# Feed-forward layers in seven stretches instead of five, with 26 instead of 22 row pairs of half B multiplied by slabs

## The chip, the cores and the metric

The kernel runs on one core of one Trainium2 chip. The metric is the time of one execution in microseconds on the device. The engines are called as in the profile: PE (matmul; PEld is its weight load), DVE (vector), ACT (scalar), POOL (GpSimd) and SP (Sync, which here only issues DMAs).

## What is computed

A decoder trunk of two layers for 256 tokens of width 2048, in float32. Each layer has a mixer and then a feed-forward part; this case is about the feed-forward part, which takes two thirds of the time:

```python
def squared_relu_mlp(h, w1, w2):
    z = jax.nn.relu(h @ w1)          # (256 x 2048) @ (2048 x 8192)
    return (z * z) @ w2              # (256 x 8192) @ (8192 x 2048)

for i in range(DEPTH):               # DEPTH = 2
    ...
    x = x + squared_relu_mlp(rms_norm(x, ffn_norm[i]), w_ff1[i], w_ff2[i])
```

Every float32 operand is split into a rounded high part and a rest, and a product is formed as high x high + high x low + low x high. So each matmul of the mathematics is three on PE, and each weight that arrives needs one copy on ACT (the high part, line 178) and one subtraction on DVE (the low part, line 181).

## The kernel before

`ffn(l, ...)` computes the feed-forward part of layer `l`. Tokens stand in two tiles of 128, the hidden width 8192 in 64 chunks of 128, taken in 32 pairs.

**The up projection** has 64 tiles `("f", j)`, one a chunk (`up_tile`). A tile takes 16 weight blocks of 128 x 128. A block is one matmul 512 wide (high weights with both parts of the input, line 947) and one 256 wide (low weights, line 949). When both tiles of a pair are there, `convert` squares and splits them over the next ticks (`STEPS`; a tick is 4 blocks) and forms sums of them.

**The down projection** is done in two ways. The 2048 output columns fall into half A (the upper 1024) and half B (the lower 1024).

- *By slabs* (`slab_jobs`): for one pair and one half, a two by two scheme with seven products instead of eight. A product is three matmuls 512 wide (lines 1038 to 1040), so a pair is 21 matmuls, dealt out in four jobs with 2, 1, 2 and 2 products. The two weight rows of a pair (512 KB each, loaded by SP) are combined on the way: POOL issues a DMA that adds half of the second row to the first, DVE does one subtraction (line 209) and one sum (line 212). The seven products add up in seven PSUM banks over a whole stretch.
- *Directly* (`down_tile`): 8 tiles `("d", 3, n)` of 128 columns, blocks as in the up projection. It covers the pairs from `NB` on in half B, so each tile has 2 x (32 - 22) = 20 blocks. `add_down` scales and adds each tile's result with three DVE operations 256 wide (lines 967 to 969).

All 32 pairs of half A and the first `NB` of half B go by slabs. `PHASES` cuts this work into stretches, each with one half and a range of pairs. At a stretch's end `finish_banks` empties the seven banks with two ACT copies and seven DVE operations 512 wide, into four corners. What an earlier stretch of the same half left is added by `gather` (DMAs on POOL) and, if more is to come, stored in HBM by `park` (SP). The last sum of a half is scaled on ACT (`scale`), transposed on PE in four steps (`turn`, tile `ct`) and added to the residual by DVE (line 1119).

**Order.** `ffn_plan` writes the order out by hand: before each tile come up to `room` jobs of the current stretch (2 in the first stretch and in the first two gaps of each later one, then 4), as far as their pairs are ready, four tiles after their second up tile (`LAG`). In the last eight tiles `room` is 4 as well. `at(d, fn)` runs a function d ticks later.

**Loads.** `Feed` prepares weights up to `AHEAD` = 3 jobs before their use and loads three rows beyond that. Direct rows go through four `raw` buffers, slab rows through three `rows` buffers and, during the stage, two that the residual's tiles lend (`feed.more`: `residb`, `residc`): the residual is stored to HBM (`kept`) at the start of the stage and brought back (`reload`) in the last stretch, when no slab is in them any more. `resida`, twice as large, lends its space to two more spots for the hidden chunks (16 + 2 `spots`). SP works off its DMAs in order, so one that waits holds all behind it.

Of the kernel before, what the change touches and what calls it, by code (L numbers as in the profile page):

```python
# [18 lines left out]
P = 128  # L19
T = 256  # L20
# [85 lines left out]
class Feed:  # L106


    def __init__(self, tc, wst, wpool, rows, plan, dry):
# [9 lines left out]
        self.more, self.lent, self.turn = [], [], 0  # L119
# [6 lines left out]
    def load(self, upto):  # L126
        while self.lp < min(upto, len(self.plan.loads)):
# [6 lines left out]
            else:  # L134
                self.turn += 1
                c = self.turn % 5
                if self.more and c > 2:
                    pool, tag = self.more[c - 3]
                    self.lent.append(r)
# [45 lines left out]
    def _prepare(self, p):  # L185
# [27 lines left out]
        if p[2] == 3:  # L213
            for r in (("S", p[1], 0), ("S", p[1], 1)):
                del self.raw[r]
                if r in self.lent:
                    self.lent.remove(r)
# [77 lines left out]
NB = 22  # L295
PHASES = (("A", 0, 6), ("B", 0, 12), ("A", 6, 18), ("B", 12, 22), ("A", 18, 32))


def ffn_plan(tiles):
# [14 lines left out]
    for t, what in enumerate(tiles):  # L314
        room = 2 if phase == 0 or since < 2 else 4
        if t >= len(tiles) - 8:
            room = 4
        since += 1
        first = len(items)
        while jobs and room and ready[jobs[0][1]] <= t and jobs[0][0] == phase:  # L320
            items.append(("s", *jobs.pop(0)))
            room -= 1
            if not jobs or jobs[0][0] != phase:
                items.append(("end", phase))
                if PHASES[phase][2] == NB:
                    turns = {t + 7 + h: h for h in range(4)}
# [37 lines left out]
def program(ctx, tc, plan, dry, xT, memT, par, lam, cst, wst, yT):  # L364
# [55 lines left out]
    def resid_part(i, name):  # L420
        if i == "a":
            both = sp.tile([P, 8, T], F32, tag="resida", name=name)
            return [both[:, 0:4, :], both[:, 4:8, :]]
        return [sp.tile([P, 4, T], F32, tag=f"resid{i}", name=name)]

    resid = Halves([x for i in "abc" for x in resid_part(i, f"resid{i}")], 4)
# [411 lines left out]
    def ffn(l, xs, tag, done):  # L838
# [19 lines left out]
        def reload(first, tags):  # L858
            for i in tags:
                for x in resid_part(i, f"resid{i}{l}"):  # L860
                    resid.parts[first] = x
                    nc.sync.dma_start(x, kept[:, 4 * first : 4 * first + 4, :])
                    first += 1

        feed.more = [] if dry else [(sp, "residb"), (sp, "residc")]
        more = sp.tile([P, 4, 512], F32R, tag="resida", name=f"more{l}")
        spots += [more[:, 2 * j : 2 * j + 2, :] for j in range(2)]
# [3 lines left out]
        def take(late):  # L871
            s = min(x for x in spare if x < 16 or not late)
            spare.remove(s)
            return s
# [20 lines left out]
        def convert(i, late):  # L895
# [16 lines left out]
            def high():  # L912
                zat[i] = take(i >= 20)
# [14 lines left out]
            def sums_high():  # L928
                sat[i] = take(i > 20)
# [122 lines left out]
        part, turns = {}, []  # L1052

        def finish_banks(p):
# [4 lines left out]
            if p == len(PHASES) - 1:  # L1059
# [22 lines left out]
            if p == len(PHASES) - 1:  # L1082
                sides = ((upp, slice(0, 2)), (low, slice(2, 4)))
            old = part.pop(half, None)
# [8 lines left out]

# [696 lines left out]
```

## Time and profile before

| | us |
|---|---|
| median of 3 runs | 2015.45 (2015.44 to 2015.52) |
| profiled execution | 2016.58, of which span 2014.8 |
| up to the first feed-forward part | 252.4 |
| feed-forward of layer 0 (252.4 to 931.2) | 678.8; DVE busy 614.9, ACT 466.8 |
| between (931.2 to 1330.4) | 399.2; DVE busy 316.8, ACT 275.8 |
| feed-forward of layer 1 (1330.4 to 2010.5) | 680.1; DVE busy 612.2, ACT 462.4 |

The granted clock of PE is 1.00 in every stretch asked for. A row of the order of time reads: start, duration, engine, line, operation, output<-input, shape, count; in brackets stands idle time before it and what ended it. Matmuls overlap, so the distance of two starts, not the duration, is what one costs. A row of a window reads: its limits and length, then the busy time of each engine with its count of instructions, the granted clock, the mean busy share of the DMA engines and GB/s. A row of the waits reads: who waited for whom, us in total, how many times, the longest.

### The profile page before, as it was taken

What the parts mean: (1) busy time and instruction counts of PE and PEld (TensorE: products, weight loads), DVE (VectorE), ACT (ScalarE), POOL (GpSimd) and SP (SyncE); (2) the same over time, 40 slices, a digit from 0 to 9 for tenths busy, and PEclk for the clock granted to TensorE, in tenths of its full rate; (3) what the DMA queues carried; (4) which work ended last, traced back from release to release, by engine and by line L of the source; (5) the groups of instructions that cost most, each with busy time, mean ns of one, the idle gap of its engine ahead of it and who ended that gap; (6) DMA issues with size and microseconds to landing.
All of it is one profiled execution on the core that took longest, in us unless ns stands there. A gap on an engine that the chain in (4) does not pass through costs nothing.

```text
span 2014.8 us, 30584 instructions
## 1 busy us (share of the span) xinstructions
PE 2003.7 (99%) x10636; PEld 1709.2 (85%) x10636; DVE 1754.6 (87%) x2665; ACT 1371.6 (68%) x2209; POOL 163.3 (8%) x191
## 2 busy tenths in 40 slices
PE   9999999999999999999999999999999999999999
PEld 7888888888888888888888889888888888888887
DVE  8888778999999999998775698878899999999987
ACT  7765467676666677667665698557676677677664
POOL 0001300000001110000000000320000000101000
PEclk9999999999999999999999999999999999999999
DMA  9566767777878888756656545666777877878775
GB/s 310 183 195 201 231 205 214 239 226 227 247 230 241 250 224 264 214 180 214 227 183 195 187 143 174 216 222 213 234 233 221 247 223 231 264 232 240 243 214 157
DMA packets 135370, 442.95 MB, mean 220 GB/s; under 512 B 15344, under 2 KB 18416, under 8 KB 135216
## 3 DMA queue, kind: packets, MB, share of 16 engines
q1 hardware_dynamic: 117216, 406.39, 60.4%
q0 software_dynamic: 17856, 34.61, 10.4%
q8 instruction: 83, 1.36, 0.3%
q14 instruction: 71, 0.58, 0.1%
q10 hardware_dynamic: 144, 0.01, 0.0%
HBM read 425.61 MB, written 12.58 MB: 217 GB/s over the span
## 4 chain that ended last, share of the span: by engine, by line
PE 55%; DVE 1%; DMA 1%; ACT 1%; issue 0%; POOL 0%; ACTq 0%; DVEq 0%; POOLq 0%
PE x_bank L947 13%; PE x_bank L949 6%; PE p L1038 5%; PE p L1040 5%; PE p L1039 5%; PE wo L522 3%; PE k L553 3%; PE v L553 3%; PE q L553 3%; PE ff L947 2%; PE wo L524 1%; PE mv L553 1%; PE mk L553 1%; PE ff L949 1%; DMA c_b<-part 1%; DVE lo_ring L181 1%
## 5 line engine op out<-in xcount | busy, mean ns | idle before, releaser
L181 DVE TENSOR_TENSOR lo_ring<-raw,hi_ring 128x512 fp32r<-128x512 f32 (+1 forms) x685 | 570.1, 847 | 128.4 <-ACT hi_ring L178 121.3
L178 ACT CAST hi_ring<-raw 128x512 fp32r<-128x512 f32 (+1 forms) x685 | 497.5, 741 | 231.4 <-PE wo L522 67.2
L181 DVE TENSOR_TENSOR lo_ring<-slab,hi_ring 128x1024 fp32r<-128x1024 f32 (+1 forms) x324 | 334.5, 1042 | 48.9 <-ACT hi_ring L178 47.3
L178 ACT CAST hi_ring<-slab 128x1024 fp32r<-128x1024 f32 (+1 forms) x324 | 293.5, 907 | 112.9 <-DVE slab L212 56.9
L149 POOL DMA_DIRECT2D slab<-in_w x108 | 93.6, 867 | 1575.9 <-DVE lo_ring L181 468.8
L947 PE MATMUL x_bank<-fx,hi_ring 128*128 128x512 f32 x664 | 209.2, 395 | 0.0
L522 PE MATMUL wo<-cat,hi_ring 128*128 128x512 f32 x512 | 161.6, 396 | 0.0
L178 ACT CAST slot<-slab 128x1024 fp32r<-128x1024 f32 x108 | 113.4, 1050 | 68.0 <-PE x_bank L947 62.8
L181 DVE TENSOR_TENSOR slot<-slab,slot 128x1024 fp32r<-128x1024 f32 x108 | 131.8, 1220 | 21.7 <-ACT slot L178 21.2
L949 PEld LDWEIGHTS x_bank<-fx,lo_ring 128*128 128x128 f32 x664 | 124.7, 188 | 29.4
L947 PE MATMUL x_bank<-fx0b,hi_ring 128*128 128x512 f32 x472 | 148.2, 395 | 0.0
L961 ACT COPY room<-x_bank 128x512 f32<-128x512 f32 x118 | 68.9, 584 | 99.2 <-PE x_bank L949 99.1
L212 DVE TENSOR_TENSOR slab<-slab,slab 128x1024 f32<-128x1024 f32 x108 | 131.6, 1218 | 0.4
L949 PE MATMUL x_bank<-fx,lo_ring 128*128 128x256 f32 x664 | 130.8, 278 | 0.0
L524 PEld LDWEIGHTS wo<-cat,lo_ring 128*128 128x128 f32 x512 | 96.0, 188 | 22.0
L949 PEld LDWEIGHTS x_bank<-fx0b,lo_ring 128*128 128x128 f32 x472 | 88.7, 188 | 21.0
L947 PEld LDWEIGHTS x_bank<-fx,hi_ring 128*128 128x128 f32 x664 | 103.0, 189 | 2.2
L524 PE MATMUL wo<-cat,lo_ring 128*128 128x256 f32 x512 | 101.7, 278 | 0.0
L178 ACT CAST slot<-raw 128x1024 fp32r<-128x1024 f32 (+1 forms) x76 | 74.1, 976 | 28.6 <-PE x_bank L947 21.9
L181 DVE TENSOR_TENSOR slot<-raw,slot 128x1024 fp32r<-128x1024 f32 (+1 forms) x76 | 85.9, 1132 | 8.0 <-ACT slot L178 7.9
L949 PE MATMUL x_bank<-fx0b,lo_ring 128*128 128x256 f32 x472 | 92.7, 278 | 0.0
L947 PE MATMUL x_bank<-fx0a,hi_ring 128*128 128x512 f32 x280 | 88.0, 395 | 0.0
(561 smaller groups left out, 4787.9 us busy)
## 6 DMA issues: line engine op xcount, KB each, us to landing
raw<-in_w SPq DMA_DIRECT2D x508, 512.0 KB, 4.5
slab<-in_w SPq DMA_DIRECT2D x216, 512.0 KB, 3.8
slab<-in_w POOLq DMA_DIRECT2D x108, 256.0 KB, 5.0
part<-room SPq DMA_DIRECT2D x6, 512.0 KB, 4.7
kept<-resida SPq DMA_DIRECT2D x4, 512.0 KB, 4.6
room<-part POOLq DMA_DIRECT2D x4, 512.0 KB, 8.6
resida<-kept SPq DMA_DIRECT2D x4, 512.0 KB, 7.5
memraw<-in_mem SPq DMA_DIRECT2D x4, 512.0 KB, 3.9
```

What stands on the lines that cost most here:

```text
L149: self.nc.gpsimd.dma_start(t[:, 512:1024], self.wst[other, :, 512:1024], accum_op=ALU.add)
L178: cast = self.nc.scalar.copy(hi, src)
L181: self.nc.vector.tensor_sub(lo, src, hi.bitcast(F32))
L212: add(two, t.unsqueeze(1).to_broadcast([P, 2, 512]), two)
L522: nc.tensor.matmul(ps, hi, xs[:, k, :], start=first and j == 0, stop=False)
L524: nc.tensor.matmul(ps[:, T : 2 * T], lo, xs[:, k, 0:T], start=False, stop=last and j == len(ks) - 1,)
L553: nc.tensor.matmul(ps[t], a, b, start=i == 0 and j == 0, stop=i == NK - 1 and j == 2)
L947: nc.tensor.matmul(ps, hi, src(k), start=k == ks[0], stop=False)
L949: nc.tensor.matmul(ps[:, T : 2 * T], lo, src(k)[:, 0:T], start=False, stop=k == ks[-1])
L1038: nc.tensor.matmul(ps, al, hi[:, s], start=i == begin, stop=False)
L1039: nc.tensor.matmul(ps, ah, hi[:, s], start=False, stop=False)
L1040: nc.tensor.matmul(ps, ah, lo[:, s], start=False, stop=i == end - 1)
```

## The change

It does the following.

1. `NB` goes from 22 to 26: four more pairs of half B by slabs; the eight direct tiles shrink from 20 to 12 blocks.
2. `PHASES` has seven stretches instead of five, with 2 to 11 pairs each; half A and half B alternate as before.
3. `room` becomes 5 instead of 4 in every second gap before an up tile, from the third gap of a stretch on.
4. The residual's tiles are four of one size (`resida` to `residd`), and all four lend their space: seven slab buffers in turn. The two extra `spots` go. Before the last stretch a and b are taken out of the turn; in it a, b and later c, d are brought back.
5. Half A, parked for the last time by the third stretch from the end, is scaled before it is parked. In the last stretch the parked sum is loaded into two free spots (`fetched`, SP), and two fused DVE operations 1024 wide scale the new sum and add the parked one, in place of a gather by POOL and a scaling on ACT. The four turns come 7 to 10 ticks after the stretch's end instead of 13 to 16.
6. The turns of half B stand before tiles 60 to 63.
7. Behind layer 0 the later squares run one a tick instead of two, the statistics they feed at tick 36 instead of 28, and the splits of `x_mx` every third tick from 50 on instead of every second from 30 on.

```diff
-                c = self.turn % 5
-                if self.more and c > 2:
+                c = self.turn % (3 + len(self.more))
+                if c > 2:
...
-NB = 22
-PHASES = (("A", 0, 6), ("B", 0, 12), ("A", 6, 18), ("B", 12, 22), ("A", 18, 32))
+NB = 26
+PHASES = (
+    ("A", 0, 2), ("B", 0, 6), ("A", 2, 11), ("B", 6, 16), ("A", 11, 21), ("B", 16, 26), ("A", 21, 32)
+)
+LAST = len(PHASES) - 1
...
         room = 2 if phase == 0 or since < 2 else 4
-        if t >= len(tiles) - 8:
-            room = 4
+        if room == 4 and since % 2 and what[0] == "f":
+            room = 5
...
-        feed.more = [] if dry else [(sp, "residb"), (sp, "residc")]
-        more = sp.tile([P, 4, 512], F32R, tag="resida", name=f"more{l}")
-        spots += [more[:, 2 * j : 2 * j + 2, :] for j in range(2)]
+        feed.more = [] if dry else [(sp, f"resid{i}") for i in "abcd"]
...
-            old = part.pop(half, None)
+            old = part.pop(half, None) if p < LAST else None
...
+            if p == LAST:
+                for t, side in enumerate((upp, low)):
+                    stt(
+                        side, side, r2c[0][:, t : t + 1], fetched[t].bitcast(F32),
+                        ALU.mult, ALU.add,
+                    )
+                for h in range(4):
+                    at(7 + h, lambda h=h: turn(h))
                 return
-            at(11, scale)
-            for h in range(4):
-                at(13 + h, lambda h=h: turn(h))
+            if old is not None:
+                at(10, gather)
+            if not whole:
...
+                at(6 if old is None else 17, park)
+                if p == LAST - 2:
+                    at(15, scale)
+                return
...
+                    if (p, i, j) == (LAST - 1, NB - 2, 3):
+                        feed.more = feed.more[2:]
+                    if (p, i, j) == (LAST, 23, 3):
+                        reload("ab")
+                    if (p, i, j) == (LAST, 28, 3):
                         feed.more = []
-                    if (p, i, j) == (4, 31, 1):
-                        assert not feed.lent
-                        reload(2, "bc")
+                        for t in range(2):
+                            fetched.append(spots[take()])
+                            nc.sync.dma_start(
+                                fetched[t].bitcast(F32), part["A"][:, 2 * t : 2 * t + 2, :]
+                            )
+                    if (p, i, j) == (LAST, 31, 1):
+                        reload("cd")
...
-        at(18 + n // 2, lambda n=n: later_square(n))
+        at(18 + n, lambda n=n: later_square(n))
...
-        at(30 + 2 * n, lambda n=n: split_gain(x_mx[:, n, :], resid[:, n, :], gcol(G_MIX + 16 + n)))
+        at(50 + 3 * n, lambda n=n: split_gain(x_mx[:, n, :], resid[:, n, :], gcol(G_MIX + 16 + n)))
```

Where instructions move, at three places.

First SP, at the end of the last stretch of layer 0; `raw` and `slab` are weight rows, `resid..<-kept` brings the residual back. Before:

```order
L147 DMA raw_7794<-in_w 128x1024
L862 DMA residb_7966<-kept_2627 128x1024
L147 DMA raw_7870<-in_w 128x1024
L862 DMA residc_7968<-kept_2627 128x1024
L147 DMA raw_7889<-in_w 128x1024
L147 DMA slab_7820<-in_w 128x1024
L147 DMA raw_7891<-in_w 128x1024
```

And now:

```order
L147 DMA slab_7866<-in_w 128x1024
L147 DMA slab_7922<-in_w 128x1024
L147 DMA raw_7951<-in_w 128x1024
L862 DMA residc_8038<-kept_2628 128x1024
L147 DMA raw_7963<-in_w 128x1024
L147 DMA raw_7965<-in_w 128x1024
L147 DMA raw_7985<-in_w 128x1024
L862 DMA residd_8040<-kept_2628 128x1024
```

Before, the last slab row stood behind the reloads; now the last slab rows stand ahead of them, and only direct rows behind. The reloads of a and b and the two fetches of the parked sum stand further up in the same stretch, among slab and direct rows.

Second DVE, at the end of the last stretch of layer 0, from the third seventh-part operation on; `c_a` and `c_b` are the corners, `p_..` the banks, `lo_ring` and `slot` the low parts of weights. Before:

```order
L1074 TENSOR_TENSOR c_b<-c_a,p_6727 128x512
L1075 TENSOR_TENSOR c_a<-c_a,p_6729 128x512
L1076 TENSOR_TENSOR c_a<-c_a,c_b 128x512
L181 TENSOR_TENSOR lo_ring<-raw_7891,hi_ring 128x512
L1077 TENSOR_TENSOR c_a<-c_a,p_6730 128x512
L1078 TENSOR_TENSOR c_b<-c_b 128x512
L969 TENSOR_TENSOR resida_7154<-resida_7154,room_2625 128x256
L1079 TENSOR_TENSOR c_b<-c_b,p_6731 128x512
L181 TENSOR_TENSOR lo_ring<-raw_7904,hi_ring 128x512
```

And now:

```order
L1070 TENSOR_TENSOR c_a<-c_a,p_7128 128x512
L1071 TENSOR_TENSOR c_a<-c_a,c_b 128x512
L964 TENSOR_TENSOR resida_7387<-resida_7387,room_2626 128x256
L1072 TENSOR_TENSOR c_a<-c_a,p_7129 128x512
L1073 TENSOR_TENSOR c_b<-c_b 128x512
L411 SCALAR_TENSOR_TENSOR c_a<-c_a,d_x,zb_2625 128x1024
L1074 TENSOR_TENSOR c_b<-c_b,p_7130 128x512
L181 TENSOR_TENSOR slot_2627<-raw_7965,slot_2627 128x512
L411 SCALAR_TENSOR_TENSOR c_b<-c_b,d_x,zb_2625 128x1024
```

The same seven sums, now with the two fused operations (line 411) among them, ahead of the next low parts.

Third PE, at the first transposes (`ct`) of half A in layer 0. Before, they came after 52 direct blocks behind the last slab job, in the last rows of which they stood so:

```order
L947 MATMUL ff<-za_2623,hi_ring 128x512 x2
L949 MATMUL ff<-za_2623,lo_ring 128x256 x2
L1116 MATMUL ct<-const,c_a 128x128
L1116 MATMUL ct<-const,c_b 128x128
L1116 MATMUL ct<-const,c_a 128x128
L1116 MATMUL ct<-const,c_b 128x128
```

Now they follow one tile of 12 blocks (`x_bank`) and these rows of the next (`ff`):

```order
L942 MATMUL ff<-za_2624,hi_ring 128x512 x2
L944 MATMUL ff<-za_2624,lo_ring 128x256 x2
L942 MATMUL ff<-za_2624,hi_ring 128x512 x2
L944 MATMUL ff<-za_2624,lo_ring 128x256 x2
L942 MATMUL ff<-zb_2625,slot_2627 128x512 x2
L942 MATMUL ff<-za_2624,hi_ring 128x512 x2
L1102 MATMUL ct<-const,c_a 128x128 x3
```

So 16 whole blocks and four high halves, where 52 blocks were.

78 lines of the change are left out of this document (30 added, 48 removed).

## The prediction

> **What bounds the kernel now.** I read the page first, then windows of the feed-forward stage, then the order of time inside it, and last the waits of the tensor and Sync engines there.
>
> ```profile
> span 2014.8 us, 30584 instructions
> PE 2003.7 (99%) x10636; PEld 1709.2 (85%) x10636; DVE 1754.6 (87%) x2665; ACT 1371.6 (68%) x2209; POOL 163.3 (8%) x191
> ```
>
> PE (the tensor engine) is busy all the time, but busy time counts overlapping matmuls, so the price of work is the distance from one start to the next. These rows give it for one up-projection tile (16 blocks, direct) and the four slab jobs of one pair behind it (21 matmuls):
>
> ```profile
> 599.72 0.62 PE L947 MATMUL x_bank<-fx0a,slot 128*128 128x512 f32 x2
> ...
> 605.28 0.40 PE L1038 MATMUL p<-hi_ring,zb 128*128 128x512 f32 x1
> 605.51 0.39 PE L1039 MATMUL p<-hi_ring,zb 128*128 128x512 f32 x1
> ...
> 610.07 0.63 PE L947 MATMUL x_bank<-fx0a,hi_ring 128*128 128x512 f32 x2
> ```
>
> The tile takes 605.28 - 599.72 = 5.56 us (0.348 a block), the pair 610.07 - 605.28 = 4.79 us (0.228 a matmul, and 605.51 - 605.28 = 0.23). Nothing waits in between: PE's own work sets the time. DVE (the vector engine) is next. Two such gaps in a row, and one change of stretch:
>
> ```profile
> core 0: us, PE busy (x) PEld busy (x) DVE busy (x) ACT busy (x) POOL busy (x), PEclk, DMA share, GB/s
> 459.30:480.00 20.70, 20.70 (x108) 17.59 (x107) 19.01 (x23) 14.22 (x19) 1.73 (x2) 1.00 0.77 227
> 740.60:754.20 13.60, 13.54 (x75) 11.31 (x74) 13.60 (x17) 8.41 (x11) 3.51 (x4) 1.00 0.91 220
> ```
>
> In the steady gaps DVE works 19.01 of 20.70 us (92%); at the change of stretch it works all 13.60. There it costs PE something:
>
> ```profile
> 747.32 0.39 PE L1040 MATMUL p<-lo_ring,za 128*128 128x512 f32 x1
> 747.77 0.50 PE L1038 MATMUL p<-hi_ring,za 128*128 128x512 f32 x1
> 748.11 0.40 PE L1039 MATMUL p<-hi_ring,za 128*128 128x512 f32 x1
> 748.34 0.64 PE L947 MATMUL x_bank<-fx0a,slot 128*128 128x512 f32 x2
> ```
>
> The distances are 0.45 and 0.34 instead of 0.23, together 0.33 us late, and I take 0.45 for a whole change, since the jobs behind it show a little more. The larger stalls of the stage lie in its last stretch, one in each layer's end:
>
> ```profile
> PE ct L1116 <- ACT room L961: 1.8, 1, 1.8
> PE p L1040 <- DVE slot L181: 0.6, 1, 0.6
> PE p L1040 <- DVE lo_ring L181: 0.4, 1, 0.4
> 1944.82 6.01 DMA raw<-in_w
> SPq L147 <- DVE slab L212: 17.7, 3, 7.7
> ```
>
> The first row is layer 0 (1.8 us, a transpose waiting for the bank that ACT had not yet emptied). The next two are layer 1; the chain of waits puts the first of them behind a weight row that took 6.01 us to land, and the last row says why it was asked for late: the Sync queue stood 17.7 us in three waits for slab buffers. With the pipeline's restart these two cost about 2.0 us. So the whole end-of-stage loss is 1.8 + 2.0 = 3.8 us now.
>
> **The change, part by part.** *Four more pairs by slabs, in both layers.* In half B of the columns a pair done directly is two blocks in each of eight down tiles, 16 blocks, as much as the tile above: 5.56 us. By slabs it is 21 matmuls, 4.79 us. Eight pairs: 8 x (5.56 - 4.79) = 6.2 us less PE work. That is exact so long as PE stays the bound.
>
> By the Trainium skill ("TensorE: Matmul & The Clock Gate", Back-to-back issue gap) an isolated matmul takes N/2.4 + 2.5 ns, which would be 215.8 and 109.2 ns here: 5.20 us for the tile, 4.53 for the pair, and a gain of 5.4 us in place of 6.2. The rows are slower than the page on both sides, and the sum goes by the rows; the sustained 131 ns that the same section gives for N = 512 is shown by no row here, where 0.23 us repeats.
>
> *Four and five jobs a gap.* The price on DVE comes from starts that follow each other without idle time:
>
> ```profile
> 1937.45 1.22 DVE L181 TENSOR_TENSOR slot<-slab,slot 128x1024 fp32r<-128x1024 f32 x1 [0.26 <-ACT slot L178]
> 1938.59 0.68 DVE L181 TENSOR_TENSOR lo_ring<-slab,hi_ring 128x512 fp32r<-128x512 f32 x1
> 1939.19 1.22 DVE L212 TENSOR_TENSOR slab<-slab,slab 128x1024 f32<-128x1024 f32 x1
> 1940.33 0.42 DVE L967 TENSOR_TENSOR room<-room 128x256 f32<-128x256 f32 x1
> 1940.66 0.69 DVE L181 TENSOR_TENSOR lo_ring<-raw,hi_ring 128x512 fp32r<-128x512 f32 x1
> ```
>
> So 1024 wide costs 1.14 us, 512 wide 0.60, 256 wide 0.33. A pair needs four of the first and two of the second: 5.76 us, or 1.44 a job against PE's 1.20. Two gaps with nine jobs instead of eight are then 19.01 + 1.44 = 20.45 of 20.70 + 1.20 = 21.90 us: 93%. DVE keeps up; I cost the quicker pace itself at nothing, and its cover is that 7%.
>
> *Seven stretches instead of five.* Each end adds seven 512-wide operations, 7 x 0.60 = 4.2 us of DVE, and what parks and gathers. Now four changes stand in a layer, one of them at two jobs a gap, where nothing is late; then six, one of them likewise. Two full changes more a layer, four in all, at 0.45 us: +1.8 us. Bounds: 0 (at the gentle pace nothing shows) and 4 x 1.0, if at 93% DVE needs twice as long to recover.
>
> *The end of the stage.* Per layer the last stretch is 9 up tiles, 3 down tiles of 12 blocks and 11 pairs. PE: 9 x 5.56 + 3 x 4.17 + 11 x 4.79 = 115.2 us. DVE for an up tile is two 1024-wide splits (2.28) and half of a conversion, which these rows and three 512-wide ones make (with 0.09 off each for the overlap):
>
> ```profile
> L904 DVE TENSOR_TENSOR room<-room 128x512 f32<-128x512 f32 x19 | 13.0, 683 | 0.0
> L923 DVE TENSOR_TENSOR room<-room 128x256 f32<-128x256 f32 x20 | 8.4, 419 | 0.1
> L926 DVE TENSOR_TENSOR room<-room 128x128 f32<-128x128 f32 x20 | 5.8, 291 | 0.6
> L922 DVE TENSOR_TENSOR room<-room 128x128 f32<-128x128 f32 x20 | 5.7, 284 | 0.0
> ```
>
> That is (1.80 + 0.33 + 0.20 + 0.20)/2 = 1.27, so 3.55 a tile. A down tile is three splits and three adds, 3 x 0.60 + 3 x 0.33 = 2.8; four turned sums 2.4; the burst of the stretch before 4.2. Sum: 9 x 3.55 + 3 x 2.8 + 11 x 5.76 + 6.6 = 110.3, 96% of PE's time. The same sum for the last stretch now (11 up tiles, 4 down tiles of 20 blocks with five splits each, 14 pairs) is 142.3 of 156.1, 91%. So this is the place that gets tighter. Seven row buffers work the other way: the 17.7 us of Sync waits above were for two to five. The two may cancel; I take 2.0 us a layer, 4.0 against 3.8 now: +0.2. Bounds: 0 and 8 us.
>
> *First half parked scaled.* This removes the gather before the last sums:
>
> ```profile
> 907.05 11.69 DMA c_b<-part
> L409 DVE SCALAR_TENSOR_TENSOR mring<-memraw,param,mring 128x256 fp32r<-128x256 f32 x16 | 7.5, 472 | 0.0
> ```
>
> The chain of waits passes through those 11.69 us, but PE had 52 direct blocks (18.1 us) to do meanwhile. Instead, DVE does two fused 1024-wide operations. No row shows one: four times the 256-wide form above is 1.9 us, the plain 1024-wide one 1.14; I take 1.3, 2.6 us a layer. The first transpose needs the sum about 4.3 us after the last slab job (copy 0.6, five operations) and stands behind some 18 direct blocks, 6.5 us: hidden, cost 0. If the cover went, 2.6 us.
>
> *Later squares and mix inputs in the next stage* (two places in the tick list). The memory projection behind layer 0 loses time now, here 1.36 us instead of 0.23:
>
> ```profile
> 953.68 0.39 PE L553 MATMUL mv<-lo_ring,mring 128*128 128x512 f32 x1
> 955.04 0.73 PE L553 MATMUL mk<-hi_ring,mring 128*128 128x512 f32 x2 [0.96 <-ACT hi_ring L178]
> ```
>
> That stall comes before the squares, so spreading them does not reach it, while a shorter end brings DVE there with more left over. I take 0, between -1.5 and +2.
>
> **Sum:** -6.2 + 1.8 + 0.2 + 0 = -4.2 us. The profiled execution took 2016.58 us (span 2014.8 and 1.8 around it) and would become 2012.4. The median of the runs, 2015.45, is 1.1 us below that execution, so the forecast is 2015.45 - 4.2 = **2011.2 us**.
>
> **The rivals.** *DVE becomes the bound at the end.* From the last up tile to the end of the slab jobs stand 13 jobs and 3 down tiles: PE 13 x 1.20 + 12.5 = 28.1 us, DVE 13 x 1.44 + 8.4 + 2.5 (the last conversion) = 29.6. If it arrives there with no lead, it is 1.5 us late in each layer, and a boundary more tightly met costs as much again as I took for it (0.2): 3.4 us, 2014.6. For it: the 96%. Against it: the windows show 92% with distances of 0.23 throughout.
>
> *The end loses nothing.* More buffers and no gather end the late rows: -3.8 - 0.2 against the sum, 2007.2. For it: both stalls above trace back to rows or banks that were late, not to work that was too much.
>
> *Slower: the Sync queue.* All weight rows are issued by Sync in order, and now two reloads in two places and two fetches of parked sums stand among them in the last stretch of each layer. A reload that waits for a slab buffer holds every weight row behind it. At four places (two a layer) a row that takes 6.01 us to land meets a lead of three jobs, 3.6 us: 2.4 us each, 9.6 in all, 2020.8. It decides for "slower" from 2.05 us a place. For it: the 6.01 us row. Against it: reloads stand in the queue now and cost at most one stall of that kind in two layers.
>
> ```profile
> 503.00:510.00 7.00, 6.94 (x37) 5.55 (x36) 7.00 (x10) 4.06 (x5) 0.86 (x1) 1.00 0.98 310
> ```
>
> By the Trainium skill ("Trainium Kernel Development and Optimization", Key Constraints) transfers of all queues share the same 16 DMA engines, so a fetch slows weight rows whichever queue issues it; the window agrees, with the engines at 0.98.
>
> *The change doesn't do what it says:* parking scaled saves a transfer for which PE never waited. That is already in the sum, at 0.
>
> **How the numbers follow.** A measurement of this kernel can tell about 0.2% from no change, 4.0 us: below 2011.4 is faster, above 2019.5 slower. Chances: forecast 0.52 (own range 2009.5 to 2013), DVE-bound end 0.22, end without loss 0.18, Sync queue 0.08. The forecast lies just past the border: 0.29 of its 0.52 are faster. Faster: 0.29 + 0.18 = 0.47; same: 0.23 + 0.22 = 0.45; slower 0.08. The range for 8 in 10 reaches into both neighbours: 2007.0 to 2015.0.
>
> **What would show it.** Right: 812 matmuls (58 pairs x 7 products x 2 layers) instead of 756 at each of the three slab lines, distances still 0.23 and tiles still 5.56 us; DVE near 20.4 of 21.9 us in a pair of gaps; six changes of stretch a layer with some 0.4 us each; no wait of the turned sums for a gather. Wrong: distances above 0.23 throughout the five-job gaps (DVE-bound), PE waits on rows behind a reload or a fetch (Sync), or an idle PE at the last transposes (the fused sums not hidden).

## The result and the profile after

The changed kernel takes 2031.1 us (median of four runs, 2030.5 to 2034.6) against 2015.5 us for the kernel of before: a ratio of 1.0087, 95% interval 1.0075 to 1.0099. It is slower by 15.7 us, where 4.2 us faster was forecast. The page of the changed kernel:

```profile
span 2029.3 us, 30490 instructions
...
PE 2013.5 (99%) x10548; PEld 1695.9 (84%) x10548; DVE 1797.7 (89%) x2713; ACT 1376.7 (68%) x2213; POOL 175.0 (9%) x207
```

PE has 88 instructions fewer and is "busy" 9.8 us longer. Its price of work has not changed, as these rows of its order in time show (x2 is two matmuls in a row):

```profile
655.65 0.63 PE L942 MATMUL x_bank<-fx0b,hi_ring 128*128 128x512 f32 x2
...
656.35 0.63 PE L942 MATMUL x_bank<-fx0b,hi_ring 128*128 128x512 f32 x2
...
657.75 0.39 PE L1033 MATMUL p<-hi_ring,za 128*128 128x512 f32 x1
...
658.44 0.39 PE L1033 MATMUL p<-hi_ring,za 128*128 128x512 f32 x1
```

Two direct blocks take 656.35 - 655.65 = 0.70 us and three slab matmuls 658.44 - 657.75 = 0.69, as before. So the extra time stands between the instructions. To find it I took, for every matmul of the two feed-forward stages, the distance to the next start less the undisturbed distance, and summed it from one end of a stretch to the next ("lost time", in us; loss behind a change of stretch counts to the stretch that follows). The stretches stand in their order, five before and seven after:

```
                       stretches of layer 0                    of layer 1
before   .3  .4  .9  .9           last 3.4   .6 1.0 1.1 1.2           last 3.2   sum 13.4
after    .2  .2 1.5 2.6 2.6 3.6   last 8.0   .3  .2 1.6 2.6 2.6 3.6   last 7.3   sum 37.4
```

The sums have 0.4 us behind the last stretch in them. PE loses 24.0 us more; the two stages, each from its first matmul to the end of its last, are together 17.6 us longer (688.2 + 687.7 against 678.6 + 679.7). So the work without the losses is 6.4 us shorter, near the 6.2 forecast, and a loss four times as large lies on top. (What one takes for the undisturbed distance, and whether the smallest excesses count, moves each sum by a few us and their difference by one or two, so the 6.4 is good to about 2 us.) The stage between the two is 3.1 us shorter. The windows show where the loss arises: two pairs of steady gaps, then the end of that stretch, then one change.

```profile
core 0: us, PE busy (x) PEld busy (x) DVE busy (x) ACT busy (x) POOL busy (x), PEclk, DMA share, GB/s
520.00:541.90 21.90, 21.90 (x111) 18.23 (x110) 19.88 (x23) 14.18 (x19) 1.73 (x2) 1.00 0.86 236
541.90:563.70 21.80, 21.80 (x110) 17.88 (x109) 20.84 (x24) 14.71 (x19) 1.73 (x2) 1.00 0.68 205
563.70:579.00 15.30, 15.30 (x77) 12.70 (x76) 12.64 (x15) 11.74 (x16) 1.02 (x2) 1.00 0.64 226
579.00:600.00 21.00, 20.78 (x107) 16.54 (x106) 21.00 (x27) 13.53 (x18) 4.21 (x5) 1.00 0.85 211
```

In the steady gaps DVE works 19.88 and 20.84 us, on either side of the 20.45 forecast, and PE's busy time has no hole. The distances show more: even in these two windows they add up to 0.7 us lost. Two such places in the next stretch, 79 and 81 us behind its change:

```profile
660.93 0.48 PE L1035 MATMUL p<-slot,za 128*128 128x512 f32 x1
661.24 0.39 PE L1033 MATMUL p<-slot,za 128*128 128x512 f32 x1
...
663.52 0.50 PE L1033 MATMUL p<-hi_ring,za 128*128 128x512 f32 x1
663.86 0.39 PE L1034 MATMUL p<-hi_ring,za 128*128 128x512 f32 x1
```

The distances are 0.31 and 0.34 us instead of 0.23. If only distances count that are at least 0.02 us too long, the fourth and the fifth stretch of layer 0 lose 2.1 us each: 1.0 and 1.2 us in their first three gaps, where the change is, and 1.1 and 1.0 from the sixth gap on.

At the change DVE works all 21.00 us and PE falls behind. The rows there (time, duration, in brackets the idle time before and what ended it):

```profile
587.18 0.58 ACT L956 COPY room<-x_bank 128x512 f32<-128x512 f32 x1
...
587.41 0.39 PE L1035 MATMUL p<-lo_ring,za 128*128 128x512 f32 x1
587.65 1.57 ACT L178 CAST hi_ring<-slab 128x1024 fp32r<-128x1024 f32 x2
587.69 0.69 DVE L1074 TENSOR_TENSOR room<-room,p 128x512 f32<-128x512 f32 x1
...
587.81 0.73 PE L942 MATMUL x_bank<-fx0a,slot 128*128 128x512 f32 x2
...
588.75 0.50 PE L1033 MATMUL p<-hi_ring,za 128*128 128x512 f32 x1 [0.21 <-ACT hi_ring L178]
...
589.09 0.40 PE L1034 MATMUL p<-hi_ring,za 128*128 128x512 f32 x1
```

Two direct matmuls at 587.81 are followed only at 588.75, by a slab product that waited for its cast; the cast stood behind a copy. DVE is still at the sums of the change (L1074). The page's bracket says 0.21 us, the distances say more: a wait that starts while a matmul is in flight shows only in part, so distances are the safer reading. In the last stretch the stalls are longer:

```profile
854.62 1.05 ACT L178 CAST hi_ring<-raw 128x1024 fp32r<-128x1024 f32 x1 [0.51 <-PE p L1034]
...
855.81 0.39 PE L1035 MATMUL p<-slot,za 128*128 128x512 f32 x1
856.01 1.04 ACT L178 CAST slot<-slab 128x1024 fp32r<-128x1024 f32 x1 [0.33 <-PE p L1034]
...
857.11 0.50 PE L1033 MATMUL p<-slot,za 128*128 128x512 f32 x1 [0.91 <-ACT slot L178]
```

From 855.81 to 857.11 PE does nothing new. The cast that it needs started at 856.01, when PE itself had freed a place in the ring for it, behind a cast for a direct row that comes later. In the kernel of before the prefetch is ahead more often. The waits of ACT over the whole span, first of before and then of after, show it:

```profile
ACT room L961 <- PE x_bank L949: 99.1, 69, 2.3
ACT slot L178 <- PE x_bank L947: 84.7, 47, 2.4
...
ACT hi_ring L178 <- DVE slab L212: 56.9, 48, 3.6
```

```profile
ACT hi_ring L178 <- DVE slab L212: 156.9, 66, 3.8
...
ACT room L956 <- PE x_bank L944: 49.5, 35, 3.3
ACT slot L178 <- PE x_bank L942: 48.0, 31, 2.9
```

(Engine and line, what it waited for: us in total, times, longest.) An ACT that waits for PE is ahead of it; an ACT that waits for DVE, here for the third weight sum of a pair at L212, has DVE behind. The two have changed places.

### The profile page after: what moved, and what is told of

The parts are those of the page before. It is cut to its first block, busy times and chain, and to the rows that moved or that the text cites. A ratio compares the mean times of both kernels' runs of the same rounds, so it can differ in the third digit from the quotient of the medians.

```text
span 2029.3 us, 30490 instructions
## 1 busy us (share of the span) xinstructions
PE 2013.5 (99%) x10548; PEld 1695.9 (84%) x10548; DVE 1797.7 (89%) x2713; ACT 1376.7 (68%) x2213; POOL 175.0 (9%) x207
## 4 chain that ended last, share of the span: by engine, by line
PE 94%; DVE 3%; ACT 1%; issue 1%; DMA 1%; SPq 0%; DVEq 0%; ACTq 0%
PE x_bank L942 21%; PE x_bank L944 11%; PE p L1033 9%; PE p L1035 8%; PE p L1034 8%; PE wo L521 6%; PE wo L523 3%; PE ff L942 3%; PE q L552 3%; PE k L552 3%; PE v L552 3%; PE u L521 2%; PE mk L552 2%; PE mv L552 2%; PE ff L944 1%; DVE lo_ring L181 1%
## 5 line engine op out<-in xcount | busy, mean ns | idle before, releaser
L181 DVE TENSOR_TENSOR lo_ring<-raw,hi_ring 128x512 fp32r<-128x512 f32 (+1 forms) x657 | 551.8, 852 | 92.9 <-ACT hi_ring L178 86.7
L178 ACT CAST hi_ring<-raw 128x512 fp32r<-128x512 f32 (+1 forms) x657 | 480.4, 744 | 212.1 <-PE wo L521 62.3
L178 ACT CAST hi_ring<-slab 128x1024 fp32r<-128x1024 f32 (+1 forms) x350 | 312.9, 905 | 180.2 <-DVE slab L212 156.9
L181 DVE TENSOR_TENSOR lo_ring<-slab,hi_ring 128x1024 fp32r<-128x1024 f32 (+1 forms) x350 | 361.6, 1046 | 46.2 <-ACT hi_ring L178 44.6
L942 PE MATMUL x_bank<-fx,hi_ring 128*128 128x512 f32 x688 | 218.7, 396 | 1.0 <-ACT hi_ring L178 0.9
L212 DVE TENSOR_TENSOR slab<-slab,slab 128x1024 f32<-128x1024 f32 x116 | 141.8, 1222 | 0.3
L942 PE MATMUL x_bank<-fx0b,hi_ring 128*128 128x512 f32 x384 | 120.7, 396 | 0.0
L523 PEld LDWEIGHTS wo<-cat,lo_ring 128*128 128x128 f32 x512 | 96.2, 188 | 21.9
L1033 PE MATMUL p<-hi_ring,zb 128*128 128x512 f32 x274 | 109.7, 401 | 1.3 <-ACT hi_ring L178 1.1
L1035 PE MATMUL p<-lo_ring,zb 128*128 128x512 f32 x274 | 106.2, 397 | 1.7 <-DVE lo_ring L181 1.7
L1034 PE MATMUL p<-hi_ring,zb 128*128 128x512 f32 x274 | 107.0, 392 | 0.0
L942 PE MATMUL x_bank<-fx0a,hi_ring 128*128 128x512 f32 x304 | 97.7, 396 | 0.5 <-ACT hi_ring L178 0.2
```

The source lines that it names most:

```text
L178: cast = self.nc.scalar.copy(hi, src)
L181: self.nc.vector.tensor_sub(lo, src, hi.bitcast(F32))
L212: add(two, t.unsqueeze(1).to_broadcast([P, 2, 512]), two)
L523: nc.tensor.matmul(ps[:, T : 2 * T], lo, xs[:, k, 0:T], start=False, stop=last and j == len(ks) - 1,)
L942: nc.tensor.matmul(ps, hi, src(k), start=k == ks[0], stop=False)
L1033: nc.tensor.matmul(ps, al, hi[:, s], start=i == begin, stop=False)
```

## The experiments

The times are medians; the kernel of before took 2014.4 to 2015.2 us beside them. The theories carry letters: **V**, DVE has too little room; **Q**, the Sync queue stands at a park; **O**, order; **M** and **L**, two readings of V, come later.

### Which engine: four kernels

Without DVE's add of L212:

```diff
-            add(two, t.unsqueeze(1).to_broadcast([P, 2, 512]), two)
+            pass
```

> The changed kernel without VectorE's add of L212, the third weight sum of each half pair (1.14 us, 58 of them a layer; the outputs of the feed-forward then use a weight that is not the sum). TensorE's stream and every transfer stay as they are. It takes some 66 us a layer from VectorE, so about 8% of its time in the stretches. Theory V (VectorE has too little slack: each change of stretch puts a burst of 4.2 us on it, and it catches up only over some gaps): the changes of stretch lose at most 1 us each instead of 2.6, the last stretch at most 3.5 us instead of 7.7, so 2011 to 2018 us, 13 to 20 below the changed kernel's 2031.1. Theory Q (the Sync queue stands at a park that waits for a gather, and weight rows come late): TensorE's losses stay, 2028 to 2031 us. Theory O (the order of TensorE's instructions at a change costs it the time whatever VectorE does): 2026 to 2031 us.

Measured 2007.0 us, 24 below the changed kernel, and lost time 12.5 us instead of 37.4. All but an ordinary rest of the loss goes when DVE has 9% less to do (577 us busy in layer 0's stage instead of 635), with PE's matmuls and the transfers the same. (In the traces 640 of the 10548 matmuls stand in another place, many of them around the late ones of the changed kernel.) V stands, and O falls as it was told, with an order that costs PE the time whatever DVE does. One reserve: the add is also a link between a row and its cast, so without it that chain is shorter, too. The thinner burst and the late fives, further down, leave the chain as it is. The window behind the same change of stretch, which now begins 1 us after it instead of 3 us ahead of it:

```profile
579.00:600.00 21.00, 21.00 (x116) 18.07 (x116) 18.88 (x25) 13.64 (x19) 4.35 (x5) 1.00 1.00 294
```

Without the gathers of the middle stretches:

```diff
-            if old is not None:
-                at(10, gather)
```

> The changed kernel without the gathers of the middle stretches (twelve accumulating DMAs a layer on the Pool queue; the sums of the earlier stretches are then missing from the feed-forward's outputs). The parks stay, but wait for nothing but VectorE's sums, so the Sync queue no longer stands for 7 to 8 us at a park. Theory Q: four changes of stretch a layer fall from 2.6 us to the 0.9 us of before, 8 x 1.7 = 14 us less: 2015 to 2019 us. Theory V: no change that matters, 2029 to 2032 us. If both share it: 2020 to 2027 us.

Measured 2033.4 us, a little above what V gave. The Sync queue's waits for gathers (in 400 to 800 us 15.9, 10.7 and 3.5 us) are gone and nothing is won: Q falls. Those rows, of the changed kernel:

```profile
SPq L1093 <- DMA c_x<-part: 15.9, 2, 8.1
SPq L1093 <- DMA c_y<-part: 10.7, 2, 7.6
...
SPq L1093 <- DMA room<-part: 3.5, 2, 1.9
```

A thinner burst, with four of the seven sums left out:

```diff
-            add(x2, x2, x1)
+            if p == LAST:
+                add(x2, x2, x1)
...
```

> The changed kernel with four of the seven sums at the end of each stretch but the last left out (the feed-forward's outputs lack the terms of two products): the burst on VectorE at a change falls from about 4.2 us to 1.8 us, six times a layer. All else stays. Theory V: a change loses about 1 us instead of 2.6, and the last stretch, which keeps its burst, some 1 us less: 12 x 1.2 to 12 x 1.6 = 14 to 19 us less, 2012 to 2019 us; if the burst is only part of the lag, 2020 to 2026 us. Theories Q and O: 2029 to 2031 us.

Measured 2025.5 us, 5.6 less: the fourth to sixth stretches lose 1.8, 1.8 and 2.5 us instead of 2.6, 2.6 and 3.6. The burst counts, but for a third of the 14 to 19 us that V gave it alone, and in the range told for a part of the lag; the last stretches keep 8.8 and 6.4. By place (distances at least 0.02 us too long), what goes is the loss in the first three gaps, from 1.0 to 1.2 us down to 0.3. The loss from the sixth gap on stays, and so does one in the fourth gap of the sixth stretch, 1.0 us before and 0.9 now.

The table of ticks behind layer 0 alone, on the kernel of before:

```diff
-        at(18 + n // 2, lambda n=n: later_square(n))
+        at(18 + n, lambda n=n: later_square(n))
...
```

> The kernel of before with nothing of the change but the table of ticks after the first layer's feed-forward (the squares one tick each from 18 on, the column sums at 36, the split of x_mx at 50 + 3n). Between the two feed-forwards the changed kernel's trace is 2.9 us shorter (396.3 against 399.2). If that comes from the table: 2012 to 2013.5 us, faster than before by 2 to 3.5 us. If it comes from what the last stretch leaves over at its end: 2015 to 2016 us.

Measured 2014.7 us, ratio 1.000 (0.999 to 1.001): the table is worth nothing by itself. The 3.1 us by which the stage between is shorter come from something else. In versions of the changed kernel with the same code there this stage takes 396.3 us (as in the changed kernel; half of the adds, below), 398.1 (no add) and 398.4 (24 pairs, below), against 399.4 before. So some 2 us of it go with how the feed-forward leaves off; the rest is open.

### How the loss grows with DVE's load: four kernels

The kernel of before without the same add:

> The kernel of before without VectorE's add of L212 (the same cut as in the run without the add of the changed kernel; the feed-forward's outputs then use a weight that is not the sum). It is the control: what VectorE's relief is worth where the changes of stretch already lose only 0.9 us. Theory V, with a threshold (the kernel of before lies under it, the changed one over it): of before's 13.4 us of lost time only the two last stretches (3.4 and 3.2 us) can fall to the 2.0 us seen without the add, so 2 to 3 us less, 2011.5 to 2013.5 us; the changed kernel without the add then stays 4 to 6 us faster than this one, which is the gain that the prediction forecast for TensorE's work. Against it, a cost that the add has by itself wherever it stands: some 20 us less here too, 1990 to 1997 us.

Measured 2007.5 us, 7.3 less, lost time 3.8 instead of 13.4. A miss for the threshold: the kernel of before had DVE losses as well, at its changes and in its last stretches. And the changed kernel without the add (2007.0) is no faster than this one. Its work is shorter, but it still loses 12.5 - 3.8 = 8.7 us more: 6.2 us of work buys nothing even with this part of DVE's load gone.

Every second add left out:

```diff
-            add(two, t.unsqueeze(1).to_broadcast([P, 2, 512]), two)
+            if p[1] % 2:
+                add(two, t.unsqueeze(1).to_broadcast([P, 2, 512]), two)
```

> The changed kernel with the add of L212 left out in every second half pair (29 of 58 a layer; outputs of the feed-forward wrong in those products). VectorE has half of the relief, some 33 us a layer, 4% of its time in the stretches. If the loss goes with VectorE's load in a straight line, half of the 24 us: 2018 to 2020 us. If it is a threshold (a burst that the lead just does not cover), most of the loss goes with the first half of the relief: 2008 to 2013 us.

Measured 2013.9 us: half of the relief brings 17.2 of 24.1 us, between the line and the threshold. Lost time goes 37.4, 19.2, 12.5.

Half of that relief, or all of it, with nothing left out, by GpSimd:

```diff
-            sub(t, t, ra[:, 512:1024])
+            self.nc.gpsimd.tensor_sub(t, t, ra[:, 512:1024])
```

> The changed kernel with the subtraction of L209 (512 wide, one a half pair) on GpSimd instead of VectorE; all is computed as before. VectorE loses 58 x 0.60 = 35 us a layer, the same relief as the run with half of the adds. GpSimd's 256-wide forms take 0.6 to 1.0 us in the changed kernel's rows, so 1.3 to 2.0 us for one, of 10.9 us that two gaps of a pair last: it has the time. Theory V: as the run with half of the adds, 2008 to 2019 us, and if it is below 2012 it beats both kernels. If GpSimd's later end of the sum, or what it takes from VectorE's reads, costs as much as it frees: 2025 to 2035 us.

```diff
-            add(two, t.unsqueeze(1).to_broadcast([P, 2, 512]), two)
+            self.nc.gpsimd.tensor_add(two, t.unsqueeze(1).to_broadcast([P, 2, 512]), two)
```

> The changed kernel with the add of L212 (1024 wide, one a half pair) on GpSimd instead of VectorE; all is computed as before. VectorE has the whole relief of the run without the add (66 us a layer). By four times GpSimd's 256-wide rows the add takes 2.4 to 4.0 us there instead of 1.2, and the queue that issues the accumulating weight transfers stands behind it that long. Theory V: if the later sum is hidden by the lead of three jobs (3.6 us), as without the add, 2007 to 2011 us, faster than before; if the weight transfers behind it or the later sum show, 2012 to 2030 us.

Measured 2137.7 and 2215.9 us, 106 and 185 us slower than the changed kernel and far outside all that was told. GpSimd had the time (rows below: 1.8 and 2.8 us each, within the forecasts), but what it does DVE does not do meanwhile; this is taken up in the last section.

```profile
L209 POOL TENSOR_TENSOR slab<-slab 128x512 f32<-128x512 f32 x116 | 206.6, 1781 | 672.5 <-DVE slot L181 337.2 <-DVE lo_ring L181 334.8 <-DMA raw<-in_w 0.5
```

```profile
L212 POOL TENSOR_TENSOR slab<-slab,slab 128x1024 f32<-128x1024 f32 x116 | 321.8, 2774 | 384.6 <-DVE slot L181 235.5 <-DVE lo_ring L181 139.5 <-ACT zb L910 4.8
```

### Lead or load: four kernels

Theory L: what covers DVE is the lead of the split halves over PE, a few jobs deep, not the mean slack. Theory M: the mean load alone. First the five-job gaps, moved to the end of each stretch (in the changed kernel the first of them is the fourth gap of a stretch):

```diff
-        if room == 4 and since % 2 and what[0] == "f":
+        if room == 4 and since > 5 and what[0] == "f":
```

> The changed kernel with the five-job gaps of a stretch at its end (the 7th gap on) instead of every second gap from the 4th; each stretch has the same jobs and ends at the same tile, and all is computed. Theory L (what covers VectorE is not its mean slack but the lead of the split halves over TensorE, which never exceeds some 4 to 5 us and is 0.2 us at the last part of a pair; the burst after a change uses it up, and nothing but gaps with little to do refill it): two jobs less, 2.9 us of VectorE, stand in the gaps that refill it, so a middle change falls from 2.6 to about 1.5 us; 8 changes, and little in the last stretch, where the fives then fall together with the turned sums: 2019 to 2027 us. If the five-job gaps cost by themselves wherever they stand: 2029 to 2034 us.

Measured 2021.8 us, 9.3 less with the same work on every engine. That refutes M. Layer 0's middle stretches lose 1.0 to 2.2 us, its last stretch 3.7 instead of 8.0, which the expectation did not have. It is the main part: by distances at least 0.02 us too long, the two last stretches fall from 14.3 to 5.8 us, the third to sixth of both layers from 16.7 to 12.8, with little of that in layer 1 (8.4 to 7.4). Then a shorter look-ahead:

```diff
-SLOTS, AHEAD, LOADS, KOFF, RAWS = 6, 3, 3, 2, 4
+SLOTS, AHEAD, LOADS, KOFF, RAWS = 6, 2, 3, 2, 4
```

> The changed kernel with the halves of the weights split two jobs ahead instead of three (AHEAD 2), all else the same, VectorE's work too. Theory L: a lead that is shorter by one job (1.2 us of TensorE's time, out of 4 to 5) leaves nothing at a change of stretch and makes the last part of every pair late, by 0.2 to 1 us: 2045 to 2130 us. Theory M (VectorE's mean load alone sets the loss, the lead plays no part): 2029 to 2034 us.

Measured 2020.7 us: both theories miss, and L by its sign. Two jobs ahead is 10.4 us better than three. Then a longer ring on both kernels, which had to give up a raw buffer:

```diff
-SLOTS, AHEAD, LOADS, KOFF, RAWS = 6, 3, 3, 2, 4
+SLOTS, AHEAD, LOADS, KOFF, RAWS = 7, 4, 3, 2, 3
```

> The changed kernel with a ring of seven slots for the split halves instead of six, four jobs ahead instead of three, and for the room three raw buffers for rows instead of four; all is computed. VectorE's work is the same. Theory L: a lead longer by up to one job (1.2 us) takes from each change of stretch up to 1.2 of its 2.6 us, and some from the last stretch: 2012 to 2024 us. If the third raw buffer gone makes rows late, that eats it: 2025 to 2040 us. Theory M: 2029 to 2034 us.

> The kernel of before with the same seven slots, four jobs ahead and three raw buffers. Theory L: of its 13.4 us of lost time 9.6 went with VectorE's relief; a longer lead should win a part of them, 2010 to 2014 us, faster than before. If the row buffer that is gone costs: 2016 to 2025 us. Theory M: 2014 to 2016 us.

Measured 2032.6 us (nothing won) and 2033.1 us (18.7 slower than the kernel of before). ACT's waits for raw rows (`hi_ring`), over the whole span, were 24.4 us in the kernel of before and 13.8 in the changed kernel, and are now these, of the changed kernel and of the kernel of before with seven slots:

```profile
ACT hi_ring L178 <- DMA raw<-in_w: 67.1, 58, 4.6
```

```profile
ACT hi_ring L178 <- DMA raw<-in_w: 87.6, 58, 8.6
```

The 2033.1 us of the second kernel lie above every range told for it. Three things changed at once, so this says little of the ring; it says that the raw buffer was needed.

### Where the loss arises: six kernels

Both cures together, one job ahead, and two jobs ahead on the kernel of before (diffs as above, with AHEAD 2, 1 and 2):

> The changed kernel with both: halves split two jobs ahead, and the five-job gaps at the end of each stretch; all is computed. Each alone took 9 to 10 us off the 2031.1. If they remove different losses (the look-ahead the order in which VectorE's work stands, the late fives the load right behind a change): 2011 to 2015 us. If they remove the same (mostly the loss of the last stretch): 2018 to 2022 us.

> The changed kernel with the halves split one job ahead. Theory O (the nearer VectorE's and ScalarE's queues hold work to the order in which TensorE needs it, the less waits): 2012 to 2021 us. Theory L with an optimum at two (one job, 1.2 us of TensorE's work, does not cover a cast of 1.05 and a subtraction of 1.2 us behind it): 2040 to 2200 us.

> The kernel of before with the halves split two jobs ahead instead of three. Of its 13.4 us of lost time 9.6 go with VectorE's relief. If the shorter look-ahead removes the same share as in the changed kernel (13 of 37 us): 4 to 5 us less, 2009 to 2011 us. If it helps only where VectorE is overrun: 2013 to 2016 us. If the lead was what held before together: 2018 to 2030 us.

Measured 2020.7, 2057.7 and 2019.1 us. The cures remove largely the same loss (lost time 24.1 us, against 26.6 and 24.3 alone). One job is too short (the stretches from the third on lose more; in layer 0 the fourth to sixth 5.4, 5.3 and 6.0, the last 9.4), so L is right on that side, and the other idea told there, that nearer queues keep DVE and ACT to the order that PE needs, fails. And before is slower by 0.18% (0.09 to 0.28) with two, in the range told for a lead that held it together. So of the look-aheads tried two is the best for the changed kernel, and three for the kernel of before.

The add left out in the last stretches alone:

```diff
-            add(two, t.unsqueeze(1).to_broadcast([P, 2, 512]), two)
+            if p[1] % 58 < 47:
+                add(two, t.unsqueeze(1).to_broadcast([P, 2, 512]), two)
```

> The changed kernel without the add of L212 in the last stretch of each layer alone (11 of 58 half pairs; those products use a weight that is not the sum). If the loss of the last stretch (8.0 and 7.3 us) arises from its own load, it falls to some 2.5 us and the others keep theirs (2.6, 2.6, 3.6): 2019 to 2023 us. If it is carried in from the stretches ahead: 2026 to 2031 us.

Measured 2024.5 us, between the two ranges told. The last stretches lose 3.2 and 2.9 instead of 8.0 and 7.3, the others exactly what they did (2.6, 2.6, 3.6). The last stretch's loss is its own, and each stretch can be read alone.

Two pairs back (24), in the same seven stretches, first with the gaps of the change, then with late fives:

```diff
-NB = 26
+NB = 24
-    ("A", 0, 2), ("B", 0, 6), ("A", 2, 11), ("B", 6, 16), ("A", 11, 21), ("B", 16, 26), ("A", 21, 32)
+    ("A", 0, 2), ("B", 0, 6), ("A", 2, 11), ("B", 6, 15), ("A", 11, 21), ("B", 15, 24), ("A", 21, 32)
```

> The changed kernel with 24 pairs by slabs in half B instead of 26, in the same seven stretches (the fourth and the sixth have 9 half pairs instead of 10), with the same four and five jobs a gap; all is computed. TensorE does 4 x 0.77 = 3.1 us more than in the changed kernel, VectorE 4 x 5.76 us less of slab work and 4 x 2.28 us more of direct splits. If stretches and pace make the loss: 37 us of lost time stay, 2032 to 2035 us. If the two pairs overrun it: half of what the change lost comes back, 2019 to 2026 us.

> The same 24 pairs with the five-job gaps only from the 7th gap of a stretch on; all is computed. By the late fives' 9 us with 26 pairs: from the 2032 to 2035 us of the run before, 2022 to 2026 us; if fewer pairs and late fives leave only the losses of the kernel of before (13 us and two more changes a layer, 4 to 6 us) against 3.1 us less work: 2014 to 2018 us.

Measured 2030.8 us and 2015.2 us. Taking the pairs back brings nothing (4.5 us less lost, 3.1 us more work). Of the same 24 pairs, jobs and stretches, the order of the gaps decides over 15.6 us: lost time 32.9 against 17.7. By distances at least 0.02 us too long, the last stretches fall from 10.9 to 3.4 us and the third to sixth from 15.2 to 7.4. ACT's waits in the second one are again those of a prefetch that is ahead:

```profile
ACT room L956 <- PE x_bank L944: 109.1, 74, 2.1
ACT slot L178 <- PE x_bank L942: 109.0, 53, 3.3
ACT hi_ring L178 <- DVE slab L212: 96.2, 61, 3.8
```

At 2015.2, in the second range told, it equals the kernel of before (1.0003, 0.9993 to 1.0013). No version with all of its work done beats that kernel.

## Why the prediction was wrong

**Eight pairs, -6.2 us: right.** 812 matmuls stand at each slab line, as forecast, direct blocks and slab matmuls cost what they did, and the stages without their losses are 6.4 us shorter.

**The pace, 0 us: this step failed**, and took two more with it. It said "DVE keeps up; I cost the quicker pace itself at nothing, and its cover is that 7%." The 7% was worked out for steady gaps, and DVE's busy time there agrees (19.88 and 20.84 of 21.9 us). But it is a mean. Even in such gaps single matmuls come late, about 1 us a stretch, and it was used as cover for changes and for a last stretch that are not steady. The runs price the order of the gaps directly: with the fives at the end of each stretch 9.3 us go with 26 pairs and 15.6 with 24. It is not simply that the first five-job gap, the fourth of a stretch, meets the sums of the change: there the fourth and fifth stretches lose next to nothing, and where the sixth loses 1.0 us, 0.9 stay with four of the seven sums gone.

**Changes of stretch, +1.8 us: measured +15.4.** All stretches but the last lose 21.7 us, before 6.3. The step counted two new changes a layer at the old price of 0.45, with 1.0 as upper bound; but the change raised the price of the old ones too, from 0.9 to 2.6 and 3.6 us of lost time for a stretch, about half of it at the change itself. The multiplication was over four changes and should have been over all.

**End of the stage, +0.2 us: measured +8.6** (15.3 against 6.7 in the last stretches). The bound of 8 was near it, the value taken was not, because the seven row buffers were set against the tighter load. Load and order decide together: without the add in that stretch alone the two lose 6.1 us, and with the same load but late fives layer 0's loses 3.7 instead of 8.0.

**Parked scaled, 0 us: hidden as told.** The fused 1024-wide operations took 1.29 us (1.3 was estimated), and no turned sum waits for a gather.

**Later squares, 0 us: right** for the table alone (2014.7). The 3.1 us won between the stages lie outside the bound of 1.5 and stay in part unexplained.

**The rivals.** "DVE becomes the bound at the end" named the engine, and one of the two places, at 3.4 us instead of 8.6 and with the changes left out. The Sync queue, told as the slower side, was for reloads and fetches in the last stretch. Those were not tried alone, but the trace speaks against them. ACT casts every row, and it waits for rows only 2.1 us in layer 0's last stretch and 1.8 in layer 1's, while these lose 8.0 and 7.3. One stall, 1.3 us at 820 us, follows a slab row for which ACT waited 1.2 us; that row was asked for at 810.22, right at the end of a split by DVE (808.97 + 1.23) and 2.8 us after the reload ahead of it, so it had to wait for a buffer and not for the reload. What the runs tried, parks that wait for gathers, costs nothing.

**What stays open.** Late fives change two things: the load right behind a change, and whether a gap holds one whole pair (up to the sixth) or parts of two (from the fourth on, in the changed kernel). Both may cost. The late matmuls far behind a change stand in gaps with parts of two, at the end of a stretch with late fives as well; without the add about half of that loss is gone. The runs do not separate the two, and why the fourth gap of the sixth stretch loses 1.0 us and that of the fourth and fifth almost nothing is not shown. Why two jobs of look-ahead are better than three in the changed kernel is not shown. A stall like that at 856 us, where a cast for a later row stands ahead of the one that PE needs, would be shorter with less look-ahead, but that was argued, not tried. And the waits of ACT for L212 are a sign, not a price: with two jobs ahead they are as long as in the changed kernel (159.0 us), while 13 us less are lost.

## What to carry to other kernels

Slack of an engine that prepares data for the bound engine is not a mean over steady windows: take it where its extra work falls, by the distances between the bound engine's own instructions rather than by its busy time. If a change adds bursts and also speeds up the pace, price every burst again, the old ones too. Where a schedule has light and heavy gaps, try the light ones first in each stretch; here that order alone was worth 9 to 16 us, though which of its effects did it is open.

## What the runs showed of the hardware

GpSimd and DVE hardly ever run two-operand work side by side. In the kernel with GpSimd's add, 573 of DVE's 604 operations on 1024 elements in a row overlap none of GpSimd's tensor operations, and each took at most 1.23 us; the 31 that overlap took 2.30 on average. Of these 17 took 2.66 to 4.05. The other 14 took 1.22 to 1.24, and they overlap by less than 0.45 us or meet a GpSimd operation that is itself longer than its like (up to 4.50). Two examples, from the kernels with GpSimd's add and with its subtraction:

```profile
965.09 4.05 DVE L181 TENSOR_TENSOR lo_ring<-raw,hi_ring 128x1024 fp32r<-128x1024 f32 x1
965.38 2.66 POOL L212 TENSOR_TENSOR slab<-slab,slab 128x1024 f32<-128x1024 f32 x1
```

```profile
1549.70 3.07 DVE L181 TENSOR_TENSOR lo_ring<-slab,hi_ring 128x1024 fp32r<-128x1024 f32 x1
1550.05 1.62 POOL L209 TENSOR_TENSOR slab<-slab 128x512 f32<-128x512 f32 x1
```

The first operation's 4.05 us is about its own 1.22 and GpSimd's 2.66 together (3.88), the second's 3.07 about 1.22 + 1.62 = 2.84: DVE stands while GpSimd works. The Trainium skill ("GPSIMD Engine Reference", Specifications) says that GpSimd shares its interfaces to the on-chip memory with VectorE, with contention when the latter has two inputs there; the rows agree and give its size. So moving a two-operand operation from a DVE that is full to GpSimd freed nothing: DVE had it to wait for, at 2.3 times the price (2.77 us against 1.22). An estimate from the rows, if DVE stands for all of it: 322 us on GpSimd in place of 142 on DVE for the add, 180 more against 185 measured, and 207 in place of 80 for the subtraction, 127 more against 106. That the later sums and transfers behind GpSimd cost nothing of their own was not tried.
